# Seven-product column pairs in a SwiGLU layer: pinned weight sums on GpSimd, sums of h as side work, Silu on ScalarE

## The chip, the cores and the metric

The kernel runs on one core of a Trainium2 chip. The metric is device time in microseconds (us) of one execution, the median of several runs. A profile is taken of one execution; in it PE is the matrix engine, PEld its weight load, DVE the vector engine, ACT ScalarE, POOL GpSimd, SP the engine that issues the DMAs. Each engine takes its instructions in the order in which the program's scheduler has put them.

## The reference

Two layers of a hybrid trunk run over 576 tokens (512 of a prompt, 64 of a sample). Each layer has a token mixer (a state-space scan beside sliding-window attention), then a gated feed-forward part. Only the feed-forward part of the second layer (layer 1) matters here:

```
h2 = rmsnorm(x, norm_ffn_g) * (1 + sc_f) + sh_f          # 1024 x 576
gate, up = split(h2 @ w_gate_up, 2)                       # 2 x 2816 columns: 22 blocks of 128 each
x = x + gt_f * ((silu(gate) * up) @ w_down)
```

Everything is float32. A weight or an activation is split into a high part (the value rounded to the PE's faster float32 form) and a low part (what is left), and a product is three matmuls: high by high, low by high, high by low.

## The kernel before

**Tokens and weights.** The tokens are cut into two halves of 288 columns (`H0`, `H1`). A weight block (`Gran`, lines 172 to 200) is 1024 rows by 128 columns, 512 KB: SP loads it into one of four `raw` buffers, ACT casts the high part `whi` (line 168), DVE or POOL subtracts for the low part `wlo` (line 169, two instructions for a whole block; `eng` says on which engine). `whi` and `wlo` have four buffers each, and a `raw` buffer is free for the next load when both parts of the block stand.

**Classic blocks.** One column block f of gate and up takes 2 weight blocks x 2 halves x 8 k x 3 = 96 matmuls of 288 columns. `by_halves` runs the first half of several blocks ahead of their second half, with the weights loaded and split twice; the first three blocks of the feed-forward part (the lead: six jobs on H0, six on H1, 24 matmuls each) run so, since the second half of h2 is made while they run. That work is the side generator `nf1`: `Norm.apply` in four parts, each a scale on DVE, the shift on DVE and ACT, a cast on ACT (`hh`), a subtraction on DVE (`hl`).

**Pairs.** In layer 1 (`WIDE`) the other blocks are `PairJob`s (lines 350 to 393): gate and up columns of one f against the two halves are a 2 x 2 block product that is done with seven products in place of eight, 7 x 4 x 3 = 84 matmuls. It needs four sums of weight blocks per pair (`ws`, lines 227 to 232: s1, s2, s3, s4, all on POOL) and sums of the halves of h2 (T1 to T4, `Norm.combine`, lines 772 to 813), high and low part each. The products go in the order of step s = 0 to 6, and `step(s)` makes high and low part of the weights: s = 0, 4, 5 straight from `raw`, s = 1, 2, 3, 6 from s2, s3, s1, s4. The low part is made on POOL for s = 4 and 5 (`POOL_LO`), on DVE else. A pair's two `raw` buffers are given back after step 6.

**Sections.** The 22 blocks run in sections (`secs`), each followed by its share of w_down (8 output blocks, `dn`).

**Gates.** SiLU is built as (tanh(x/2) + 1) x on ACT and DVE, and the missing factor 1/2 stands in the adaLN gate (line 437).

**Order.** The code emits work job by job: weights of the next job are split after a job's first part, and side generators are advanced by `pump` at their rate at each step of a job. After that a scheduler orders the instructions of each engine by its own estimate, within the data's dependencies. So where an instruction stands in its engine's queue need not be where the code says it.

Of the kernel before, what the change touches and what calls it, by code (L numbers as in the profile page):

```python
# [12 lines left out]
ALU = mybir.AluOpType  # L13
# [38 lines left out]
def hybrid_trunk(ctx: ExitStack, tc: tile.TileContext, I, O):  # L52
# [109 lines left out]

    def f32(ap):
        return ap.bitcast(F32)
# [38 lines left out]
    class PairGran(Gran):  # L203
# [13 lines left out]
        def step(self, s):  # L217

            p = self.pair
            g, u = p["gate"], p["up"]  # L220
            if s == 0:
                p["s12"], p["s34"] = (w4("ws", [128, 2, 4, 128]) for _ in range(2))
                p["hi"], p["lo"] = [], []
            s1, s2 = p["s12"][:, 0], p["s12"][:, 1]
            s3, s4 = p["s34"][:, 0], p["s34"][:, 1]
            if s == 1:
                G.tensor_tensor(out=s1, in0=u.block(1, 0), in1=u.block(1, 1), op=ALU.add)  # L227
                G.tensor_tensor(out=s2, in0=s1, in1=g.block(0, 0), op=ALU.subtract)  # L228
            if s == 2:
                G.tensor_tensor(out=s3, in0=g.block(0, 0), in1=u.block(1, 0), op=ALU.subtract)  # L230
            if s == 6:
                G.tensor_tensor(out=s4, in0=g.block(0, 1), in1=s2, op=ALU.subtract)
# [187 lines left out]
    def ada_finish(l, b, ps):  # L420
# [15 lines left out]
        if b in (2, 5):  # L436
            V.tensor_scalar(out=md[:, b], in0=md[:, b], scalar1=0.5, scalar2=None, op0=ALU.mult)
# [261 lines left out]
    class Norm:  # L699
# [47 lines left out]
        def part(self, half, k2, src, fast):  # L747
# [21 lines left out]
            if self.wide and half:  # L769
                self.combine(k2, t)  # L770

        def combine(self, k2, t):

            js = slice(2 * (k2 % 2), 2 * (k2 % 2) + 2)
            if self.wino is None:
                self.wino = {}
                for n in range(4):
                    if n == 0:
                        v = [bcs("T", [128, 4, HALF], F32R) for _ in range(2)]
                    else:  # L780
                        v = blk("T", [128, 2, 4, HALF], F32R)
                        v = [v[:, 0], v[:, 1]]
                    self.wino[f"T{n + 1}"] = v
                for i in range(2):
                    for j in range(2):
                        self.wino[f"{i + 1}{j + 1}"] = [self.hh[i][:, :, HS[j]], self.hl[i][:, :, HS[j]]]

            def parts(nm):
                return [f32(a[:, js]) for a in self.wino[nm]]

            def less(x, nm, eng, sign=1):

                o = w4("tw", [128, 2, HALF])
                h, lo = parts(nm)
                if sign == 1:
                    eng.tensor_tensor(out=o, in0=x, in1=h, op=ALU.subtract)
                    eng.tensor_tensor(out=o, in0=o, in1=lo, op=ALU.subtract)
                else:
                    eng.tensor_tensor(out=o, in0=h, in1=x, op=ALU.subtract)
                    eng.tensor_tensor(out=o, in0=o, in1=lo, op=ALU.add)  # L800
                return o

            def put(nm, x, eng):
                h, lo = self.wino[nm]
                split(h[:, js], lo[:, js], x, eng)

            if k2 < 2:
                put("T1", less(t, "11", G), V)
                return
            t2 = less(t, "T1", V)  # L810
            put("T2", t2, V)
            put("T3", less(t, "12", G), G)
            put("T4", less(t2, "21", V, -1), V)
# [23 lines left out]
    def layer(l, nrm, jobs):  # L837
# [757 lines left out]
        secs = ((0, 4), (4, 6), (10, 6), (16, 6)) if wide else ((0, 8), (8, 8), (16, 6))  # L1595
# [8 lines left out]
        def a_alloc(f, f0, nf):  # L1604
# [11 lines left out]
        def pair_evac(f, f0, nf):  # L1616
            def evac(a, b, cc, d):
# [12 lines left out]
                act(g0, a, ACTF.Tanh, scale=0.5)  # L1630
                stt(g0, g0, 1.0, a, ALU.add, ALU.mult)
# [8 lines left out]
                act(g1, u2, ACTF.Tanh, scale=0.5)  # L1640
                stt(g1, g1, 1.0, u2, ALU.add, ALU.mult)
# [5 lines left out]
        def gu_evac(f, f0, nf):  # L1647
            def evac(m, half, ps):
                h = HS[half]
                if m == 0:  # L1650
                    t = st["gate", f, half] = w2("gate", [128, HALF])
                    act(t, ps[:, 0:HALF], ACTF.Tanh, scale=0.5)
                    stt(t, t, 1.0, ps[:, 0:HALF], ALU.add, ALU.mult)
                    return
# [43 lines left out]
        for sec, (f0, nf) in enumerate(secs):  # L1698
# [8 lines left out]
            if wide:  # L1707
                jobs += [PairJob(I["w_gate_up"][l], f, lambda: st["n2"], pair_evac(f, f0, nf), f)
                         for f in range(f0 + lead, f0 + nf)]
                if lead:  # L1710
                    jobs[-1].pre = lambda: drain("nf1")
# [163 lines left out]
```

## Time and profile before

| what | value |
|---|---|
| time of the runs | 2598.99 us, median of 3 (2594.55 to 2605.43) |
| the profiled execution | 2604.75 us, of which the span from first to last instruction is 2603.0 us |
| PE / DVE / POOL / ACT busy | 96% / 67% / 48% / 43% of the span |
| mean granted PE clock | 0.985 |

The feed-forward part of layer 1 runs from about 2141 us to the end. How to read it: matmuls of one product run into one another, so that a busy PE does not say at what rate they go; what counts is how many start in a stretch, how long PE waits and for whom, and the clock it was granted in that stretch (1.00 is 2.4 GHz, and 0.5 the other level, 1.2 GHz).

### The profile page before, as it was taken

The numbers are of one execution on the slowest core, as the hardware profiler recorded it, in microseconds if no ns is written. First come the engines' busy times: TensorE is split into PE (matmuls) and PEld (weight loads), VectorE is DVE, ScalarE is ACT, GpSimd is POOL, SyncE is SP. The second block draws the span as 40 slices with busy tenths as digits, with TensorE's granted clock in tenths as the row PEclk, the third lists the DMA queues.
The fourth block names the chain that finished last, engine by engine and source line by source line (L and its number), as shares of the span: only waits on it lengthen the run. The fifth ranks groups of instructions, "written<-read, shape, count | busy, mean of one in ns | idle before, by whom it ended". The sixth has DMA issues, their size and how long they took to land.

```text
span 2603.0 us, 49408 instructions
## 1 busy us (share of the span) xinstructions
PE 2508.9 (96%) x19381; PEld 2378.2 (91%) x19381; DVE 1737.2 (67%) x3159; ACT 1107.6 (43%) x2483; POOL 1244.4 (48%) x1092
## 2 busy tenths in 40 slices
PE   7999999999999999999999999999999997999989
PEld 6888899999889999999989899999988997998989
DVE  4598676745765765655768995956376567767684
ACT  3444454443453532322355455443354454333343
POOL 3445455343225754544675555544422378436260
PEclk8999999999999999999999999999999998999999
DMA  7555523242224555445573333323312253332323
GB/s 219 156 164 149 156 86 97 83 103 71 58 61 120 158 168 166 143 154 162 155 183 103 106 91 98 107 79 87 100 50 58 85 164 89 87 92 75 89 65 86
DMA packets 464236, 294.34 MB, mean 113 GB/s; under 512 B 69220, under 2 KB 446532, under 8 KB 464004
## 3 DMA queue, kind: packets, MB, share of 16 engines
q1 hardware_dynamic: 464004, 291.18, 38.9%
q8 instruction: 153, 2.51, 0.4%
q14 instruction: 79, 0.65, 0.1%
HBM read 276.98 MB, written 13.16 MB: 111 GB/s over the span
## 4 chain that ended last, share of the span: by engine, by line
PE 70%; DVE 15%; POOL 5%; DMA 5%; issue 3%; ACT 2%; SPq 0%; ACTq 0%; POOLq 0%; DVEq 0%
PE dps L326 19%; PE dps L328 19%; PE dps L327 19%; DVE cv L155 3%; POOL wlo L169 3%; DMA raw<-in_w_gate_up_dram 2%; DVE xT L155 2%; DVE seg L158 1%; PE sc L1353 1%; PE wps L371 1%; PE pv L1416 1%; PE wps L372 1%; PE wps L369 1%; POOL ws L228 1%; PE pT L1400 1%
## 5 line engine op out<-in xcount | busy, mean ns | idle before, releaser
L169 POOL TENSOR_TENSOR wlo<-raw,whi 128x512 fp32r<-128x512 f32 (+1 forms) x670 | 957.2, 1437 | 877.9 <-ACT whi L168 746.3
L326 PE MATMUL dps<-hh,whi 128*128 128x288 f32 x2928 | 878.6, 301 | 15.5 <-ACT whi L168 14.0
L327 PE MATMUL dps<-hh,wlo 128*128 128x288 f32 x2928 | 872.1, 298 | 2.8 <-POOL wlo L169 2.8
L328 PE MATMUL dps<-hl,whi 128*128 128x288 f32 x2928 | 871.4, 298 | 1.1 <-DVE hl L158 1.1
L168 ACT CAST whi<-raw 128x512 fp32r<-128x512 f32 (+2 forms) x759 | 453.7, 601 | 510.3 <-PE dps L328 366.7
L326 PEld LDWEIGHTS dps<-hh,whi 128*128 128x128 f32 x2928 | 552.3, 189 | 38.6 <-issue 16.8
L327 PEld LDWEIGHTS dps<-hh,wlo 128*128 128x128 f32 x2928 | 553.0, 189 | 12.0 <-POOL wlo L169 5.5
L328 PEld LDWEIGHTS dps<-hl,whi 128*128 128x128 f32 x2928 | 552.8, 189 | 7.7 <-issue 5.3
L155 DVE SCALAR_TENSOR_TENSOR ada_acc<-araw,csl,ada_acc 128x1024 f32<-128x1024 f32 x98 | 152.4, 1593 | 72.1 <-DMA araw<-in_ada_w_dram 72.1
L155 DVE SCALAR_TENSOR_TENSOR cv<-u,colB,cv 128x579 f32<-128x579 f32 x144 | 146.5, 1017 | 30.0 <-ACT cv L161 22.6
L326 PE MATMUL dps<-yh,whi 128*128 128x288 f32 x512 | 153.2, 299 | 1.1 <-ACT u L948 1.1
L328 PE MATMUL dps<-yl,whi 128*128 128x288 f32 x512 | 153.9, 301 | 0.0
L327 PE MATMUL dps<-yh,wlo 128*128 128x288 f32 x512 | 152.1, 297 | 0.0
L327 PE MATMUL dps<-ah,wlo 128*128 128x288 f32 x352 | 105.6, 300 | 4.1 <-POOL wlo L169 4.1
L326 PE MATMUL dps<-ah,whi 128*128 128x288 f32 x352 | 104.2, 297 | 3.2 <-ACT ah L168 2.6
L328 PE MATMUL dps<-al,whi 128*128 128x288 f32 x352 | 104.6, 297 | 0.0
L327 PE MATMUL dps<-a,wlo 128*128 128x288 f32 x352 | 104.4, 298 | 0.0
L326 PE MATMUL dps<-a,whi 128*128 128x288 f32 x352 | 103.1, 295 | 0.0
L328 PE MATMUL dps<-a,whi 128*128 128x288 f32 x352 | 102.8, 295 | 0.0
L227 POOL TENSOR_TENSOR ws<-raw 128x512 f32<-128x512 f32 x19 | 28.0, 1475 | 155.8 <-DMA raw<-in_w_gate_up_dram 145.2
L326 PEld LDWEIGHTS dps<-yh,whi 128*128 128x128 f32 x512 | 97.4, 190 | 4.1 <-issue 1.9
L155 DVE SCALAR_TENSOR_TENSOR x<-dps,mod,x 128x288 f32<-128x288 f32 (+2 forms) x168 | 63.6, 411 | 54.1 <-PE dps L328 52.6
(372 smaller groups left out, 5484.4 us busy)
## 6 DMA issues: line engine op xcount, KB each, us to landing
raw<-in_w_in_dram SPq DMA_DIRECT2D x119, 512.0 KB
raw<-in_w_gate_up_dram SPq DMA_DIRECT2D x100, 512.0 KB
araw<-in_ada_w_dram SPq DMA_DIRECT2D x56, 512.0 KB
bc<-ac_dr SPq DMA_DIRECT2D x32, 512.0 KB
raw<-in_w_br_ssm_dram SPq DMA_DIRECT2D x32, 512.0 KB
raw<-in_w_out_dram SPq DMA_DIRECT2D x32, 512.0 KB
raw<-in_w_down_dram SPq DMA_DIRECT2D x40, 384.0 KB
raw<-in_ada_w_dram SPq DMA_DIRECT2D x24, 512.0 KB
```

Of the source, the lines that this page charges most:

```text
L155: V.scalar_tensor_tensor(out=out, in0=in0, scalar=scalar, in1=in1, op0=op0, op1=op1)
L158: V.tensor_tensor(out=out, in0=in0, in1=in1, op=op)
L168: S.copy(out=hi, in_=src)
L169: (eng or V).tensor_tensor(out=lo, in0=src, in1=f32(hi), op=ALU.subtract)
L227: G.tensor_tensor(out=s1, in0=u.block(1, 0), in1=u.block(1, 1), op=ALU.add)
L228: G.tensor_tensor(out=s2, in0=s1, in1=g.block(0, 0), op=ALU.subtract)
L326: T.matmul(ps, lhsT=wh, rhs=rh, start=a == 0, stop=False)
L327: T.matmul(ps, lhsT=wl, rhs=rh, start=False, stop=False)
L328: T.matmul(ps, lhsT=wh, rhs=rl, start=False, stop=a == nk - 1)
L369: T.matmul(ps, lhsT=wh[:, k], rhs=rh[:, k], start=first and k == 0, stop=False, skip_group_check=True)
L371: T.matmul(ps, lhsT=wl[:, k], rhs=rh[:, k], start=False, stop=False, skip_group_check=True)
L372: T.matmul(ps, lhsT=wh[:, k], rhs=rl[:, k], start=False, stop=k == 3, skip_group_check=True)
```

## The change

Four edits, all in layer 1's feed-forward part.

1. The four weight sums are put through `tc.keep_in_program_order`, so that the scheduler leaves them where the code emits them on POOL.
2. The sums of h are no longer made inside `Norm.part`. `combine` is a generator of its own, made from `hh` and `hl` (three GpSimd instructions for T3 and for T1, two on DVE for T2 and for T4, and the splits), added as side work `comb` (rate 0.75) when the H1 jobs of the lead begin and drained before the first pair.
3. Two more blocks (f = 3 and 4) are classic, and the sections are cut 6, 6, 6, 4 in place of 4, 6, 6, 6. The weights of the six H1 jobs of the lead are split on DVE in place of POOL.
4. In layer 1 the gate is one Silu on ACT, without the DVE instruction behind Tanh and without the factor 1/2.

```diff
+    pin = tc.keep_in_program_order
...
             if s == 1:
-                G.tensor_tensor(out=s1, in0=u.block(1, 0), in1=u.block(1, 1), op=ALU.add)
-                G.tensor_tensor(out=s2, in0=s1, in1=g.block(0, 0), op=ALU.subtract)
+                pin(G.tensor_tensor(out=s1, in0=u.block(1, 0), in1=u.block(1, 1), op=ALU.add))
+                pin(G.tensor_tensor(out=s2, in0=s1, in1=g.block(0, 0), op=ALU.subtract))
...
-            if self.wide and half:
-                self.combine(k2, t)
...
+        def combine(self):
...
+            for js in (slice(0, 2), slice(2, 4)):
+                part = lambda nm: [f32(a[:, js]) for a in self.wino[nm]]
...
+                def less(p, q, eng):
+                    (ph, pl), (qh, ql) = part(p), part(q)
+                    o, r = (w4("tw", [128, 2, HALF]) for _ in range(2))
+                    eng.tensor_tensor(out=o, in0=ph, in1=qh, op=ALU.subtract)
+                    eng.tensor_tensor(out=r, in0=pl, in1=ql, op=ALU.subtract)
+                    eng.tensor_tensor(out=o, in0=o, in1=r, op=ALU.add)
+                    return o
+
+                t3 = less("22", "12", G)
+                put("T3", t3, V)
+                yield
+                (h, lo), t2 = part("11"), w4("tw", [128, 2, HALF])
+                tt(t2, t3, h, ALU.add)
+                tt(t2, t2, lo, ALU.add)
+                put("T2", t2, G)
+                yield
+                (h, lo), t4 = part("21"), w4("tw", [128, 2, HALF])
+                tt(t4, h, t2, ALU.subtract)
+                tt(t4, t4, lo, ALU.add)
+                put("T4", t4, G)
+                yield
+                put("T1", less("12", "11", G), V)
+                yield
...
-        secs = ((0, 4), (4, 6), (10, 6), (16, 6)) if wide else ((0, 8), (8, 8), (16, 6))
+        secs = ((0, 6), (6, 6), (12, 6), (18, 4)) if wide else ((0, 8), (8, 8), (16, 6))
...
+        def gate(out, x):
+
+            if wide:
+                act(out, x, ACTF.Silu)
+                return
+            act(out, x, ACTF.Tanh, scale=0.5)
+            stt(out, out, 1.0, x, ALU.add, ALU.mult)
...
+                if lead:
+                    f1 += 2
+                    for j in gj[2 * lead:]:
+                        for gr in j.gr:
+                            gr.eng = V
+                    gj[2 * lead].pre = lambda: (drain("nf1"), add_side("comb", st["n2"].combine(), 0.75))
+                    jobs += gu_jobs(range(f0 + lead, f1))
+                pj = [PairJob(I["w_gate_up"][l], f, lambda: st["n2"], pair_evac(f, f0, nf), f)
+                      for f in range(f1, f0 + nf)]
+                if lead:
+                    pj[0].pre = lambda: drain("comb")
```

What the scheduler makes of it, first on POOL, among the pairs of one section. In the program before, rows of two pairs in a row (`ws` are the sums s1, s3, s2, s4, `wlo` the low parts of steps 4 and 5; the numbers tell buffers apart, so that raw_26504 and raw_26506 are gate and up of one pair, raw_26340 and raw_26379 of the pair before it):

```order
L227 TENSOR_TENSOR ws_26539<-raw_26379 128x512
L230 TENSOR_TENSOR ws_26540<-raw_26340,raw_26379 128x512
L228 TENSOR_TENSOR ws_26539<-ws_26539,raw_26340 128x512
L232 TENSOR_TENSOR ws_26540<-raw_26340,ws_26539 128x512
L169 TENSOR_TENSOR wlo_26463<-raw_26262,whi_26462 128x512
L169 TENSOR_TENSOR wlo_26482<-raw_26301,whi_26481 128x512
L227 TENSOR_TENSOR ws_26686<-raw_26506 128x512
L230 TENSOR_TENSOR ws_26687<-raw_26504,raw_26506 128x512
L228 TENSOR_TENSOR ws_26686<-ws_26686,raw_26504 128x512
L232 TENSOR_TENSOR ws_26687<-raw_26504,ws_26686 128x512
L169 TENSOR_TENSOR wlo_26613<-raw_26340,whi_26612 128x512
L169 TENSOR_TENSOR wlo_26632<-raw_26379,whi_26631 128x512
```

The low parts of one pair stand behind all four sums of the next pair. In the changed program the same engine at the same place, two pairs in a row (raw_26666 and raw_26717, then raw_26860 and raw_26862):

```order
L229 TENSOR_TENSOR ws_26894<-raw_26717 128x512
L230 TENSOR_TENSOR ws_26894<-ws_26894,raw_26666 128x512
L232 TENSOR_TENSOR ws_26895<-raw_26666,raw_26717 128x512
L171 TENSOR_TENSOR wlo_26967<-raw_26666,whi_26966 128x512
L171 TENSOR_TENSOR wlo_26986<-raw_26717,whi_26985 128x512
L234 TENSOR_TENSOR ws_26895<-raw_26666,ws_26894 128x512
L229 TENSOR_TENSOR ws_27039<-raw_26862 128x512
L230 TENSOR_TENSOR ws_27039<-ws_27039,raw_26860 128x512
L232 TENSOR_TENSOR ws_27040<-raw_26860,raw_26862 128x512
L171 TENSOR_TENSOR wlo_27112<-raw_26860,whi_27111 128x512
L171 TENSOR_TENSOR wlo_27131<-raw_26862,whi_27130 128x512
L234 TENSOR_TENSOR ws_27040<-raw_26860,ws_27039 128x512
```

Each pair's six instructions now stand together: s1, s2, s3, the two low parts, s4, and then the next pair's.

Second on DVE, where the lead goes from its H0 to its H1 jobs. Before (`nt2` is h2 in the making, `hl` its low part, `tw` and `T` the sums of h, `gate` and `a` the activation of a lead block):

```order
L158 TENSOR_TENSOR nt2_25611<-x_24756,bc_25437 128x576
L158 TENSOR_TENSOR hl_25050<-nt2_25550,hh_25048 128x2x288
L765 TENSOR_SCALAR nt2_25611<-nt2_25611,mod1_2490 128x64
L760 TENSOR_SCALAR nt2_25611<-nt2_25611,mod1_2490 128x224
L765 TENSOR_SCALAR nt2_25611<-nt2_25611,mod1_2490 128x64
L155 SCALAR_TENSOR_TENSOR gate_25697<-gate_25697,dps_25672 128x288
L169 TENSOR_TENSOR T_25450<-tw_25454,T_25449 128x576
L796 TENSOR_TENSOR tw_25558<-nt2_25550,T_25449 128x576
L158 TENSOR_TENSOR hl_25050<-nt2_25611,hh_25048 128x2x288
L797 TENSOR_TENSOR tw_25558<-tw_25558,T_25450 128x576
```

After, the same place (`wlo` here are low parts of the first H1 jobs' weights):

```order
L158 TENSOR_TENSOR nt2_25579<-x_24755,bc_25436 128x576
L171 TENSOR_TENSOR wlo_25691<-raw_25532,whi_25690 128x512
L158 TENSOR_TENSOR hl_25049<-nt2_25534,hh_25047 128x2x288
L767 TENSOR_SCALAR nt2_25579<-nt2_25579,mod1_2490 128x64
L762 TENSOR_SCALAR nt2_25579<-nt2_25579,mod1_2490 128x224
L767 TENSOR_SCALAR nt2_25579<-nt2_25579,mod1_2490 128x64
L171 TENSOR_TENSOR wlo_25695<-raw_25532,whi_25694 128x512
L171 TENSOR_TENSOR wlo_25728<-raw_25577,whi_25727 128x512
L158 TENSOR_TENSOR gate_25650<-gate_25650,dps_25662 128x288
L158 TENSOR_TENSOR hl_25049<-nt2_25579,hh_25047 128x2x288
```

The last `hl` of h2 now has three weight splits ahead of it in place of a gate instruction, a T and a tw; all sums of h stand behind it. On POOL, where four subtractions of 576 columns stood among the weight splits at this place, the first sum of h now stands behind the last low part of the H0 jobs. Ahead of 2141 us all five queues are ordered as before, save one small DVE instruction (the factor 1/2) that is gone.

## Rows read from the trace of the kernel before

**Rows 1.** The page's first line
```profile
span 2603.0 us, 49408 instructions
```

**Rows 2.** Stretches of layer 1's feed-forward: length, busy us (count) by engine, clock, DMA
```profile
2141.00:2204.00 63.00, 47.65 (x311) 45.06 (x309) 47.72 (x59) 28.22 (x56) 56.68 (x39) 0.89 0.33 95
...
2237.00:2309.00 72.00, 64.15 (x451) 62.89 (x450) 58.24 (x84) 30.80 (x61) 45.69 (x31) 0.95 0.27 76
2309.00:2369.00 60.00, 60.00 (x455) 60.00 (x454) 35.62 (x73) 20.32 (x41) 17.35 (x13) 1.00 0.32 93
2369.00:2422.00 53.00, 43.76 (x317) 42.74 (x316) 41.32 (x60) 22.72 (x46) 35.30 (x24) 0.98 0.24 68
2422.00:2486.00 64.00, 64.00 (x479) 64.00 (x478) 38.94 (x77) 21.67 (x43) 17.39 (x13) 0.99 0.32 93
2486.00:2541.00 55.00, 46.78 (x317) 45.34 (x316) 45.19 (x61) 22.46 (x46) 35.41 (x24) 0.92 0.24 69
```

**Rows 3.** PE's pair matmuls from 2141 us, one of each three like groups
```profile
L371 PE MATMUL wps<-T,wlo 128*128 128x288 f32 x304 | 92.8, 305 | 0.9 <-POOL wlo L169 0.6 <-DVE wlo L169 0.3
...
L371 PE MATMUL wps<-hh,wlo 128*128 128x288 f32 x228 | 69.9, 307 | 24.7 <-POOL wlo L169 24.7
```

**Rows 4.** PE's waits from 2141 to 2204.5 us: total, times, longest
```profile
PE dps L326 <- ACT whi L168: 13.4, 6, 5.7
PE dps L327 <- POOL wlo L169: 1.1, 2, 0.7
```

**Rows 5.** PE's waits from 2204.5 us to the end
```profile
PE wps L371 <- POOL wlo L169: 25.3, 14, 3.1
```

**Rows 6.** PE at one wait, then at the lower clock: start, duration
```profile
2258.18 0.29 PE L369 MATMUL wps<-hh,whi 128*128 128x288 f32 x1
2261.57 0.40 PE L371 MATMUL wps<-hh,wlo 128*128 128x288 f32 x1 [3.09 <-POOL wlo L169]
...
2264.10 0.44 PE L371 MATMUL wps<-T,wlo 128*128 128x288 f32 x1
2264.34 0.44 PE L372 MATMUL wps<-T,whi 128*128 128x288 f32 x1
```

**Rows 7.** POOL over the same pair: start, duration, [idle before]
```profile
2253.83 1.61 POOL L227 TENSOR_TENSOR ws<-raw 128x512 f32<-128x512 f32 x1 [5.26 <-DVE gate L155]
...
2259.81 2.95 POOL L169 TENSOR_TENSOR wlo<-raw,whi 128x512 fp32r<-128x512 f32 x2
2267.53 1.44 POOL L227 TENSOR_TENSOR ws<-raw 128x512 f32<-128x512 f32 x1 [4.77 <-DMA raw<-in_w_gate_up_dram]
```

**Rows 8.** POOL's sums and low parts from 2237 to 2309 us: busy, mean ns
```profile
L169 POOL TENSOR_TENSOR wlo<-raw,whi 128x512 fp32r<-128x512 f32 x10 | 14.8, 1504 | 0.0
...
L228 POOL TENSOR_TENSOR ws<-ws,raw 128x512 f32<-128x512 f32 x5 | 8.2, 1650 | 0.0
```

**Rows 9.** DVE's low parts of weights, 2237 to 2309 us: min/median/max ns
```profile
L169 DVE TENSOR_TENSOR wlo<-ws,whi x22: 677/692/1787, 2239.0 to 2308.1; 128x512 fp32r<-128x512 f32 x22
...
L169 DVE TENSOR_TENSOR wlo<-raw,whi x6: 677/1342/1541, 2237.0 to 2305.7; 128x512 fp32r<-128x512 f32 x6
```

**Rows 10.** DVE by form, 2141 to 2204 us, the slowest sum of h
```profile
L800 DVE TENSOR_TENSOR tw<-tw,hl 128x576 f32<-128x576 f32 x2 | 3.7, 1854 | 0.0
```

**Rows 11.** ACT: the one table load (1.3 us busy), and the first lead gate
```profile
L161 ACT ACT_TABLE_LOAD x1 | 1.3, 1283 | 0.8 <-PEq L1860 0.8
...
2145.41 0.41 ACT L161 ACTIVATE gate<-dps 128x288 f32<-128x288 f32 x1 [0.91 <-PE dps L328]
...
2147.71 0.62 ACT L168 CAST whi<-raw 128x512 fp32r<-128x512 f32 x1 [1.37 <-POOL wlo L169]
```

**Rows 12.** DVE at the end of h2's second half: start, duration
```profile
2162.21 1.41 DVE L760 TENSOR_SCALAR nt<-nt,mod 128x224 f32<-128x224 f32 x1
...
2169.60 0.30 DVE L765 TENSOR_SCALAR nt<-nt,mod 128x64 f32<-128x64 f32 x1
...
2171.53 1.83 DVE L158 TENSOR_TENSOR hl<-nt,hh 128x576 fp32r<-128x576 f32 x1
```

More of the change, by code (lines that the diff above doesn't have):

```diff
@@ L435, in ada_finish @@
                 ALU.add, ALU.mult)
-        if b in (2, 5):
+        if b == 2 or b == 5 and l not in WIDE:
             V.tensor_scalar(out=md[:, b], in0=md[:, b], scalar1=0.5, scalar2=None, op0=ALU.mult)
@@ L768, in part @@
             tt(self.hl[q][:, ks, h], t, f32(hi), ALU.subtract)
-            if self.wide and half:
-                self.combine(k2, t)
[L772 to L797, printed above, removed]
-                else:
[L799 to L813, printed above, removed]
@@ new lines, in combine, with put @@
+        def combine(self):
+            self.wino = {}
+            for n in range(4):
+                if n == 0:
+                    v = [bcs("T", [128, 4, HALF], F32R) for _ in range(2)]
+                else:
+                    v = blk("T", [128, 2, 4, HALF], F32R)
+                    v = [v[:, 0], v[:, 1]]
+                self.wino[f"T{n + 1}"] = v
+            for i in range(2):
+                for j in range(2):
+                    self.wino[f"{i + 1}{j + 1}"] = [self.hh[i][:, :, HS[j]], self.hl[i][:, :, HS[j]]]
+            for js in (slice(0, 2), slice(2, 4)):
+                part = lambda nm: [f32(a[:, js]) for a in self.wino[nm]]
+                def put(nm, x, eng):
+                    h, lo = self.wino[nm]
+                    split(h[:, js], lo[:, js], x, eng)
+                def less(p, q, eng):
[20 more added lines that the diff above has]
+                yield
@@ L1629, in evac @@
                 g0 = w2("gate", [128, HALF])
-                act(g0, a, ACTF.Tanh, scale=0.5)
-                stt(g0, g0, 1.0, a, ALU.add, ALU.mult)
+                gate(g0, a)
                 yield
@@ L1639, in evac @@
                 g1 = w2("gate", [128, HALF])
-                act(g1, u2, ACTF.Tanh, scale=0.5)
-                stt(g1, g1, 1.0, u2, ALU.add, ALU.mult)
+                gate(g1, u2)
                 tt(g1, g1, u3, ALU.mult)
@@ L1651, in evac @@
                     t = st["gate", f, half] = w2("gate", [128, HALF])
-                    act(t, ps[:, 0:HALF], ACTF.Tanh, scale=0.5)
-                    stt(t, t, 1.0, ps[:, 0:HALF], ALU.add, ALU.mult)
+                    gate(t, ps[:, 0:HALF])
                     return
@@ L1707, in layer @@
             if wide:
-                jobs += [PairJob(I["w_gate_up"][l], f, lambda: st["n2"], pair_evac(f, f0, nf), f)
-                         for f in range(f0 + lead, f0 + nf)]
+                f1 = f0 + lead
                 if lead:
-                    jobs[-1].pre = lambda: drain("nf1")
+                    f1 += 2
[8 more added lines that the diff above has]
+                    pj[0].pre = lambda: drain("comb")
+                jobs += pj
             else:
```

4 lines of the change are left out of this document (2 added, 2 removed).

## The prediction

> **What bounds the kernel now.** I read the stretches of the feed-forward part first, then PE's instructions in it, PE's waits, and last what the engines that PE waits for were doing. The part begins at 2141 us and ends with the span at 2603.0 [rows 1], so it takes 462.0. Two stretches show PE undisturbed: 455 matmuls in 60 us at a clock of 1.00 and 479 in 64 us at 0.99 [rows 2], together 124 / 934 = 0.1328 us per matmul. The pairs hold 304 x 3 + 228 x 3 = 1596 = 19 x 84 matmuls [rows 3]; by the code the lead adds 3 x 96 = 288 and w_down 22 x 8 x 2 x 3 = 1056. That is 2940, or 390.4 us. The other 71.6 us are the room. The waits of PE account for 13.4 + 1.1 in the lead [rows 4] and 25.3 in the pairs [rows 5], 39.8 in all. The clock accounts for more: at 0.89 over 63 us, the lower level held 2 x 0.11 x 63 = 13.9 us, and 7.2, 2.1, 1.3 and 8.8 in the other stretches, 33.3 together [rows 2]. At that level matmuls start 0.24 apart in place of 0.133 [rows 6], so that each such microsecond loses 0.45: 14.9. It fell after PE had waited (as after the 3.09 us ahead of these rows), and stood at 1.00 and 0.99 in the two stretches without a wait. Each wait also costs more than its length: from 2258.18 to 2261.57 are 3.39, less 0.13 for the matmul, 3.26 for a wait of 3.09 [rows 6]; 0.17 x 22 waits = 3.7. What remains, 71.6 - 39.8 - 14.9 - 3.7 = 13.2, is the end of the kernel, the transposes of the output and smaller things, and I leave it as it is.
>
> **The pairs' waits: a loop.** All 14 are for a low part made on POOL. POOL takes 13.70 us from one pair's first sum to the next one's (2253.83 to 2267.53): four sums, 5.98; two low parts, 2.95; then 4.77 idle until the weights land [rows 7]. These weights could not be loaded earlier, since their `raw` buffers are free only after the low parts, and the low parts stand behind the next pair's sums, which wait for weights. PE needs 84 x 0.1328 = 11.16 per pair, so the loop sets the pace.
>
> **The pins.** With the new order the low parts wait for nothing but their own high parts. I walk one pair, from the start of its first product, a product being 12 x 0.1328 = 1.59; a cast takes 0.62 [rows 11], POOL's low part 1.50 and its slowest kind of sum 1.65 [rows 8]. The buffer of step 4 is free at 1.59, cast at 2.2, low part at 3.7. Step 5: free at 3.19, cast at 3.8, low part at 5.3, needed only at 8.0. Then s4 at 6.95, its cast at 7.6, its low part on DVE (0.69 to 1.34, [rows 9]) by 8.3 to 8.9. Product 6 wants it at 6 x 1.59 + 0.13 = 9.7. Four hand-overs between engines may take 0.5 of the slack (my estimate), which leaves none or 0.9. The `raw` buffers come free at about 7, and 4.77 later the weights of the pair after next are there, 6 us before they are asked for. s4 is thus what is late next, and it just fits. I take 2 us of waits for all 17 pairs; the bounds are 0, and 10 if the walk is 0.6 late each time. From 25.3 to 2: **-23.3**.
>
> **The lead.** The 1.1 at its start comes before anything that moves and stays. PE then waits for casts that stand behind h2's second half in ACT's queue, and that half is held up on DVE: its shifts take 1.41 while POOL works beside them and 0.30 when it does not, and its last low part ends at 2171.53 + 1.83 = 2173.4 [rows 12]. PE without further waits would be through with the first H1 job at 2141 + 7 x 24 x 0.1328 + 2 (the 1.1, and small matmuls of the norm) = 2165. In the new order three instructions ahead of that low part are gone (0.45 to 0.75 each, about 1.9) and POOL's four subtractions beside it too, which lets some five shifts fall by 1 us each; three weight splits come in, 0.69 to 1.34 each, say 3. So 2173.4 - 1.9 - 5 + 3 = 2169.5, and with the six matmuls that need this part (0.8) the job ends at 2170.3: 5 us of waits. For the five jobs that follow, DVE has 9 splits, 2 parts of T, 4 sums of h and 4 gate instructions. At 0.69 for all but the gates (0.45) this is 12 us; at 1.34 per split and 1.85 per sum or T [rows 9, 10] and 0.8 per gate instruction, 26. PE's own time is 5 x 24 x 0.1328 = 15.9. I take the middle, 19; the first splits are done while PE waits for that last low part, so 2 us of waits. Sum 1.1 + 5 + 2 = 8, with bounds 2 and 20: **-6.5**. The rest of comb lies beside f = 3 and 4, where a weight block serves 6.4 us of PE in place of 3.2; POOL's 16 instructions (24 us at 1.50) end before the first pair wants them.
>
> The Trainium skill has a rule that speaks against this part: in "SBUF — State Buffer", section "SBUF: two separate sides", a DVE instruction with two inputs in SBUF and a GpSimd one exclude each other for the whole instruction. The trace agrees in kind, but the median split on DVE from `ws` shows no delay [rows 9]. By the rule's full price the lead is rival A.
>
> **Two more classic blocks.** 2 x (96 - 84) = 24 matmuls more, **+3.2**. The order of the sections changes no count. In the last one an output block has 24 matmuls in place of 36; its loads shrink with it (nk = 4 of 128 rows in place of 6), so nothing.
>
> **Silu.** Its activation is put at Tanh's 0.41 [rows 11]; as the upper bound the 0.62 of a cast of 512 columns, as the lower one no gain. Even 0.62 adds 0.4 us per pair to an engine that is 45% busy at most [rows 2], so nothing. DVE loses two small instructions per pair. The table is loaded once more, ahead of the first lead gate at 2145.41: 1.28 us, with 1.37 idle soon behind it [rows 11]. Hence 0, and 1.3 if that idle time is not to be had.
>
> By the Trainium skill, "ScalarE: Activation LUTs", section "What ACT_TABLE_LOAD costs", a switch is 2.66 us, the same load with a drain behind it; the sum would be up to 1.3 us higher. The row shows the load alone.
>
> **Clock and restarts.** They go with the waits: 10 of 39.8 are left, so the clock keeps 14.9 x 0.25 = 3.7 (**-11.2**; bounds 1 and 13), the restarts 1 (**-2.7**).
>
> **Sum.** 3.2 - 23.3 - 6.5 - 11.2 - 2.7 = -40.5. The profiled execution took 2604.75, 5.8 above the median of 2598.99 that the result will be held against; I take the difference from the median: 2558.5, rounded to 2558. All the low bounds together give 3.2 - 25.3 - 12.5 - 13.9 - 3.5 = -52, 2547; all the high ones give 3.2 - 15.3 + 5.5 - 1.9 - 0.5 + 1.3 = -8, 2591.
>
> **Rivals.**
> A, DVE becomes the bound of the lead. For it: 9 splits and 6 sums of h land on DVE while POOL works without a break; against it, the median of 0.69. If each of the 15 waits for a whole POOL instruction of 1.50, the five jobs take 15 x 2.19 + 4 x 0.45 = 34.7, 18.8 of waits, 24 for the lead. Then 26 us of waits remain, the clock keeps 9.7 and the restarts 2: 3.2 - 23.3 + 9.5 - 5.2 - 1.7 = -17.5, 2581.
> B, s4 is late. If POOL's instructions take 1.9, s4's low part comes about 0.5 late in each of 17 pairs: 8.5 of waits there, clock 6, restarts 3: 3.2 - 16.8 - 6.5 - 9 - 0.7 = -30, 2569.
> C, the weights are the bound and the pins only move the wait from the low parts to the sums. For it: POOL does wait 4.77 for a landing. Against it: a pair's 1 MB in 11.16 us is 94 GB/s, and 95 GB/s were moved in the lead with a DMA share of 0.33 [rows 2]. If the pair stays at 13.7, 22.6 of the 25.3 remain: 3.2 - 2.7 - 6.5 - 3.4 - 1 = -10, 2589.
> D, slower: six POOL instructions per pair are a chain by themselves now that s4 may not run ahead. It decides from about 2.3 us each, where six take 13.8, the loop's length now. At 2.6 a pair takes 15.6, PE waits 17 x 4.4 = 75 where it waited 25.3, and with the clock's part the end is some 60 later, 2660. Against it: means of 1.50 and 1.65 [rows 8].
>
> **How the numbers follow.** Forecast 0.66, A 0.15, B 0.09, C 0.06, D 0.04. What a measurement of this kernel can tell from no change is about 0.5%, 13 us, 2586 to 2612. Faster: forecast, A and B, 0.90; same: C, 0.06; slower: D, 0.04. The forecast's own range is 2545 to 2571; to hold A's place too the range is 2543 to 2583.
>
> **What would show it.** Right: no wait of PE on POOL's low parts over 1 us in the pairs, POOL no longer idle for a DMA ahead of a pair's first sum, pairs 11.2 to 11.5 apart, a clock of 0.98 or more from the first pair on, and PE at the first pair's product at about 2141 + 63.7 + 9 = 2214. Wrong: waits of PE on a DVE low part once per pair (B), long DVE splits in the lead with PE waiting for DVE (A), or pairs 13 us apart (C, D).

## The result, and the profile after

The changed kernel takes 2560.9 us (median of four runs, 2556.5 to 2563.4) where the kernel before, on the same chip, took 2600.7: a ratio of 0.985, with a 95% interval of 0.982 to 0.987. The forecast was 2558. The profiled execution took 2562.08, its span 2560.3, against 2604.75 and 2603.0.

In that execution the part before the change ran 2.8 us shorter, in the same order: PE's last matmul ahead of the lead's first wait starts at 2138.28, where it was 2141.06. I count from there: 461.9 before, 422.0 after, 39.9 less. By the prediction's terms:

| term | predicted | measured |
|---|---|---|
| waits in the pairs | -23.3 | -23.8 (25.3 to 1.5) |
| waits in the lead | -6.5 | -5.9 (14.5 to 8.6) |
| two more classic blocks | +3.2 | +3.2 (by count: 24 matmuls more) |
| clock | -11.2 | -13.3 (33.3 us at the lower level to 3.8, at 0.45 each) |
| end, behind PE's last matmul | 0 | +1.9 (4.36 to 6.26) |
| restarts, and all that is left | -2.7 | -2.0 (the remainder) |
| sum | -40.5 | -39.9 |

The waits of PE in the changed kernel from 2141 us on (line and tile, what it waited for, total, times, longest; one more of 0.7 for POOL lies at 2139):

```profile
PE dps L329 <- DVE wlo L171: 7.9, 6, 2.3
PE wps L373 <- DVE wlo L171: 1.5, 7, 0.2
```

The line of 25.3 us for POOL's low parts [rows 5] is gone, with nothing of its size in its place. Seven small waits of the pairs are now for DVE. The stretches (columns as in [rows 2]):

```profile
span 2560.3 us, 49363 instructions
...
2141.00:2188.00 47.00, 39.16 (x275) 37.57 (x273) 41.83 (x50) 24.15 (x46) 36.02 (x23) 0.96 0.43 124
...
2225.00:2290.00 65.00, 65.00 (x491) 64.90 (x490) 39.96 (x74) 22.31 (x45) 21.40 (x15) 1.00 0.32 91
2290.00:2325.00 35.00, 34.35 (x252) 33.38 (x251) 27.48 (x43) 16.71 (x37) 26.74 (x18) 1.00 0.30 84
2325.00:2397.00 72.00, 72.00 (x544) 71.90 (x543) 44.88 (x83) 25.93 (x53) 25.76 (x18) 1.00 0.32 92
...
2504.00:2560.00 56.00, 49.77 (x378) 48.95 (x376) 30.43 (x67) 21.07 (x53) 13.27 (x9) 0.97 0.28 81
```

The clock stood at 1.00 from 2188 to 2504; only the lead has time at the lower level, 2 x 0.04 x 47 = 3.8 us (the 0.97 of the last stretch comes from 2554 us on, where PE has all but ended). The DMAs moved 124 GB/s in the lead, where pairs need 84 to 92.

POOL over one pair (start, duration, idle before and its releaser), the place of [rows 7]:

```profile
2290.26 3.09 POOL L171 TENSOR_TENSOR wlo<-raw,whi 128x512 fp32r<-128x512 f32 x2 [2.76 <-ACT whi L170]
2293.31 1.29 POOL L234 TENSOR_TENSOR ws<-raw,ws 128x512 f32<-128x512 f32 x1
2294.56 1.28 POOL L229 TENSOR_TENSOR ws<-raw 128x512 f32<-128x512 f32 x1
...
2302.01 3.08 POOL L171 TENSOR_TENSOR wlo<-raw,whi 128x512 fp32r<-128x512 f32 x2 [2.76 <-ACT whi L170]
```

The two low parts come first, then s4 and the next pair's sums. Between the pairs of a section the wait for a landing is gone: POOL waits for ACT's cast. It waits for a landing only ahead of a section's first pair, while PE works on w_down: three times from 2225 us on, and PE waits for none of them. The low parts start 11.75 us apart, where the pair of [rows 7] took 13.70.

### The profile page after: what moved, and what is told of

The parts are those of the page before. It is cut to its first block, busy times and chain, and to the rows that moved or that the text cites. A ratio compares the mean times of both kernels' runs of the same rounds, so it can differ in the third digit from the quotient of the medians.

```text
span 2560.3 us, 49363 instructions
## 1 busy us (share of the span) xinstructions
PE 2496.8 (98%) x19405; PEld 2368.0 (92%) x19405; DVE 1701.0 (66%) x3112; ACT 1098.6 (43%) x2476; POOL 1217.6 (48%) x1074
## 4 chain that ended last, share of the span: by engine, by line
PE 70%; DVE 16%; POOL 5%; issue 5%; DMA 2%; ACT 2%; SPq 0%; ACTq 0%; POOLq 0%; DVEq 0%
PE dps L328 19%; PE dps L330 19%; PE dps L329 19%; DVE cv L155 3%; POOL wlo L171 3%; DVE xT L155 2%; PE sc L1354 1%; DVE seg L158 1%; PE pv L1417 1%; DVE wlo L171 1%; PE pT L1401 1%; PE sp L1067 1%; DVE ada_acc L155 1%; DVE hl L158 1%; DVE nt L158 1%
## 5 line engine op out<-in xcount | busy, mean ns | idle before, releaser
L171 POOL TENSOR_TENSOR wlo<-raw,whi 128x512 fp32r<-128x512 f32 (+1 forms) x654 | 932.0, 1434 | 932.4 <-ACT whi L170 827.6
L329 PE MATMUL dps<-hh,wlo 128*128 128x288 f32 x2992 | 889.8, 298 | 10.4 <-DVE wlo L171 7.9
L328 PE MATMUL dps<-hh,whi 128*128 128x288 f32 x2992 | 895.0, 300 | 2.0 <-ACT hh L769 1.4
L330 PE MATMUL dps<-hl,whi 128*128 128x288 f32 x2992 | 888.8, 297 | 1.4 <-DVE hl L158 1.4
L328 PEld LDWEIGHTS dps<-hh,whi 128*128 128x128 f32 x2992 | 562.7, 188 | 23.7 <-issue 16.0
L329 PEld LDWEIGHTS dps<-hh,wlo 128*128 128x128 f32 x2992 | 563.5, 188 | 20.6 <-DVE wlo L171 9.5
L330 PEld LDWEIGHTS dps<-hl,whi 128*128 128x128 f32 x2992 | 563.6, 188 | 7.9 <-issue 5.3
L171 DVE TENSOR_TENSOR wlo<-raw,whi 128x384 fp32r<-128x384 f32 (+2 forms) x101 | 86.2, 859 | 30.7 <-ACT whi L170 30.5
L330 PEld LDWEIGHTS dps<-yl,whi 128*128 128x128 f32 x512 | 96.6, 189 | 2.0 <-issue 1.8
```

The lines of the kernel that those rows point to most:

```text
L171: (eng or V).tensor_tensor(out=lo, in0=src, in1=f32(hi), op=ALU.subtract)
L328: T.matmul(ps, lhsT=wh, rhs=rh, start=a == 0, stop=False)
L329: T.matmul(ps, lhsT=wl, rhs=rh, start=False, stop=False)
L330: T.matmul(ps, lhsT=wh, rhs=rl, start=False, stop=a == nk - 1)
```

## The experiments

Five columns to compare them. The runs come from several chips, each beside runs of the kernel before on the same chip, so that medians of different kernels compare less well than ratios. "From 16,300" is the time from one matmul ahead of the lead, number 16,300 of the program, to the end of the span, in each profiled execution: it leaves out what happens ahead of the change (474.2 for the kernel before). "To the end" is the time from PE's first product of a pair to the end of the span, in each profiled execution; it is free of what happens ahead of the pairs, and kernels that are alike there agree in it within 0.4 us (345.2, 345.0, 345.3 and 344.9 for the changed kernel and three that differ in the lead alone). Pairs are from POOL's rows where they are evenly spaced, the pace of the loop. PE's own pairs reach that pace late: in the changed kernel a section's six pairs start 11.15, 11.14, 11.27, 11.75 and 11.75 apart.

| kernel | median us | ratio (interval) | from 16,300 | to the end | pairs |
|---|---|---|---|---|---|
| changed kernel | 2560.9 | 0.9846 (0.9820 to 0.9872) | 434.3 | 345.2 | 11.75 |
| pins alone | 2576.5 | 0.9902 (0.9883 to 0.9920) | 450.3 |  | 11.96 |
| no pins | 2585.2 | 0.9938 (0.9923 to 0.9953) | 458.8 | 369.7 |  |
| Tanh | 2565.1 | 0.9863 (0.9848 to 0.9877) | 436.7 | 347.3 | 11.97 |
| three classic blocks | 2571.2 | 0.9888 (0.9873 to 0.9903) | 444.3 |  |  |
| first splits on POOL | 2563.9 | 0.9857 (0.9836 to 0.9877) | 436.7 | 345.0 |  |
| all splits on POOL | 2563.8 | 0.9859 (0.9838 to 0.9879) | 437.9 | 344.9 |  |
| comb later | 2558.8 | 0.9840 (0.9819 to 0.9862) | 433.5 | 345.3 |  |
| step 6 on POOL | 2577.1 | 0.9907 (0.9887 to 0.9928) | 450.5 | 359.9 | 12.64 |
| cast later | 2559.5 | 0.9838 (0.9822 to 0.9854) | 434.2 | 343.6 | 11.62 |
| gate later | 2558.1 | 0.9839 (0.9815 to 0.9863) | 434.0 | 343.5 | 11.44 |
| four yo buffers | 2559.5 | 0.9847 (0.9833 to 0.9860) | 432.7 | 343.6 |  |
| gate later, four yo | 2557.7 | 0.9835 (0.9821 to 0.9850) | 430.1 | 341.1 | 11.44 |

**Pins alone.** The kernel before with the pins:
```
-  G.tensor_tensor(out=s1, in0=u.block(1, 0), ...)
+  pin(G.tensor_tensor(out=s1, in0=u.block(1, 0), ...))     # and s2, s3, s4
```


> The kernel before with the four pins alone. Theory (the loop of low parts, loads and sums is what the pins break): the pairs' waits on POOL fall from 25.3 to about 2, the lead keeps its 14.5, the clock gives back 8.7 of 14.9 and the restarts 2.4; 2603.0 - 34.7 is 2568 of span, ratio 0.987. Rival (the pins help only where the lead's edits have unloaded DVE and POOL): the pairs keep most of their waits, ratio above 0.995.

It came to 0.9902; from matmul 16,300 on the trace is 23.9 us shorter, where 34.7 was expected. PE's waits in that kernel (1.1 for POOL in the lead is not shown), and the stretches at its lead and behind it:
```profile
PE dps L328 <- ACT whi L170: 12.4, 5, 4.5
PE wps L373 <- DVE wlo L171: 2.2, 10, 0.3
PE wps L371 <- ACT whi L170: 2.0, 2, 1.5
```
```profile
2140.00:2208.00 68.00, 52.42 (x310) 50.23 (x309) 50.51 (x59) 28.88 (x56) 56.34 (x38) 0.82 0.30 88
2208.00:2260.00 52.00, 51.67 (x378) 51.54 (x378) 33.67 (x74) 19.74 (x43) 17.54 (x13) 0.97 0.32 92
```
The pairs' waits fell as foreseen, and the lower level went with them there: the stretch behind the lead holds 3.1 us of it and what follows none, where the pairs of the kernel before held 33.3 - 13.9 = 19.4 [rows 2]. But the lead now holds 2 x 0.18 x 68 = 24.5 us in place of 13.9, so that 27.6 of 33.3 remain in all. Of the 10.8 us that are missing, the clock makes 6: it gives back 2.6 in place of 8.7.

**No pins.** The changed kernel with
```
-    pin = tc.keep_in_program_order
+    pin = lambda i: i
```


> The changed kernel without the pins. Theory: the sums stand ahead of the low parts again, a pair takes 13.7, PE waits about 22 in 17 pairs for POOL's low parts, and with clock and restarts the time is some 31 over the changed kernel: 2592, ratio 0.997. Rival (the lead's edits and Silu brought the gain): within 5 of the changed kernel, ratio below 0.987.

0.9938, between theory and rival: the pins are worth 458.8 - 434.3 = 24.5 us here, nearly what they are worth alone, and 0.9902 x 0.9938 = 0.984 is the whole change. So the two parts simply add. PE's waits, and the stretches of the lead and of those pairs that ran in part at the lower level:
```profile
PE wps L373 <- POOL wlo L171: 19.1, 10, 3.0
PE dps L329 <- DVE wlo L171: 7.9, 6, 2.3
```
```profile
2137.00:2188.00 51.00, 42.39 (x296) 40.69 (x296) 44.76 (x55) 27.55 (x52) 38.52 (x25) 0.97 0.41 118
...
2290.00:2340.00 50.00, 43.48 (x293) 42.69 (x292) 29.98 (x48) 20.10 (x41) 27.05 (x19) 0.90 0.26 74
...
2436.00:2500.00 64.00, 61.38 (x452) 61.14 (x451) 35.36 (x69) 19.84 (x39) 21.02 (x16) 0.97 0.28 83
...
2526.00:2540.00 14.00, 11.22 (x73) 10.99 (x72) 7.18 (x13) 5.43 (x11) 6.03 (x5) 0.88 0.14 39
```
The loop is back with its waits, 19.1 us in 17 pairs, and so is the lower level in the pairs: 10.0 + 3.8 + 3.4 = 17.2 us in these three stretches, none in the others; the lead holds 3.1. So the lower level lies in the stretch in which PE waits: the pins take it out of the pairs (19.4 to 3.1 in the kernel before, 17.2 to none here), the other edits out of the lead (13.9 to 3.1 without pins, 24.5 to 3.8 with them). How much of it goes with a microsecond of wait is not fixed: 0.9 in these pairs, 0.4 in the changed kernel's lead (3.8 for 8.6), 1.6 in the lead and first pair of pins alone (24.5 for 12.4 + 1.1 + 2.0). Each is from one profile.

**Tanh.** The changed kernel with the gate as before (the factor 1/2 in the adaLN gate is back too, and not shown here):
```
-            if wide:
-                act(out, x, ACTF.Silu)
-                return
             act(out, x, ACTF.Tanh, scale=0.5)
```


> The changed kernel with the gate as before (Tanh on ACT, one more DVE instruction, the factor 1/2). Theory: nothing on the path hangs on it, 2559 to 2563, ratio 0.984 to 0.986. Rival (two DVE instructions per pair and four per lead block are on the path): 17 pairs x 2 x 0.4 = 14 us slower, ratio 0.990.

The interval of its ratio overlaps that of the changed kernel; the trace tells more. Pairs are 11.97 apart in place of 11.75, and the stretch to the end is 2.1 longer. Silu is worth some 2 us in these traces; the likely cause, not tested by itself, is that it takes two instructions off DVE, which is in the pairs' loop. The table's load was paid by nobody: PE has no wait for ACT in the changed kernel's lead (ACT there, start and duration):
```profile
2141.72 1.28 ACT L161 ACT_TABLE_LOAD   x1
2143.02 0.41 ACT L161 ACTIVATE gate<-dps 128x288 f32<-128x288 f32 x1
```
The gate takes 0.41 with Silu as it did with Tanh, and starts 0.02 behind the load.

**Three classic blocks.** f = 3 and 4 as pairs again, comb as side work beside whatever there is:
```
                 if lead:
-                    f1 += 2
```


> The changed kernel with f = 3 and 4 as pairs. Theory: 24 matmuls less (-3.2), but PE is at the first pair at about 2188 in place of 2214, while POOL has the sums of h behind it only at 2200 and the first pair's sums of weights at 2205; PE waits 12 to 17 there, the clock and restarts take 3 more: about 2573 to 2577, ratio 0.990. Rival (the sums of h hide beside any work): 2558, ratio 0.984.

0.9888, as its theory had it: 10.3 us behind the changed kernel by the medians and 10.0 in the trace, though it has 24 matmuls (3.2 us) fewer. The two largest waits of PE up to 2214 us, and the stretch in which they lie:
```profile
PE wps L371 <- ACT whi L170: 7.8, 2, 6.2
PE wps L371 <- ACT T L170: 4.4, 1, 4.4
```
```profile
2180.00:2214.00 34.00, 18.87 (x105) 16.90 (x104) 20.76 (x24) 10.96 (x20) 26.32 (x18) 0.70 0.14 39
```
PE reaches the first pair at 2180.6, stands before sums and T that POOL and ACT have not made yet, and 2 x 0.30 x 34 = 20.4 us then run at the lower level. In the changed kernel comb ends at 2200.5 and the first product starts at 2215.1. The two blocks are the cover for comb.

**Who makes the splits of the second half.** Two kernels: the splits of its first two jobs, and of all its jobs, on POOL in place of DVE (the first kernel's edit, then the second's):
```
-                    for j in gj[2 * lead:]:
+                    for j in gj[2 * lead + 2:]:
```
```
-                            gr.eng = V
+                            gr.eng = G
```


> The changed kernel with the low parts of the first two H1 jobs' weights on POOL, the other four jobs' on DVE. Theory (PE's first waits in the lead, 1.4 + 2.3 + 0.7 between 2159 and 2167, are for splits that queue in DVE among h2's own instructions, while POOL is idle half of that time): they shrink to 1 to 2, 3 us are won, comb ends 4 to 6 us later and still ahead of the first pair: 2556 to 2559, ratio 0.983 to 0.984. Rival (POOL beside DVE slows the shifts of h2 again, to 1.4 from 0.3, as before): the wait only changes its name, 2561 or more.

> The changed kernel with all six H1 jobs' splits on POOL, as before the change. Theory: POOL has 12 splits (17 us) more in the lead, comb's three-instruction sums are pushed back as far, and the sums of the first pair come at about 2222 where PE wants them at 2214: 5 to 8 us of waits at the first pair beside 5 to 10 in the lead, 2566 to 2572, ratio 0.987 to 0.989. Rival (who splits does not matter, comb alone brought the lead's gain): 2561, ratio 0.9845.

Both are 3 us behind the changed kernel by the medians, and their intervals overlap with its own. The waits change their names and hardly their length. With all splits on POOL:
```profile
PE dps L328 <- ACT whi L170: 4.1, 2, 3.5
PE dps L328 <- ACT hh L769: 2.4, 1, 2.4
PE dps L329 <- POOL wlo L171: 1.8, 2, 1.0
PE dps L329 <- DVE wlo L171: 1.6, 1, 1.6
```
9.9 us, where DVE's splits left 8.6. I had expected comb to end too late; it ended at 2206.9 (at 2200.5 in the changed kernel, whose trace runs 1.8 us behind), and the first pair at 2217.2 still found its sums. The traces say a little more than the medians: from matmul 16,300 to the first pair's product these two kernels take 91.7 and 93.0 us, where the seven with the changed kernel's lead take 89.1 or 90.6. So by these two profiles the splits on DVE are worth 1 to 4 us.

**Comb later.**
```
-  gj[2 * lead].pre = lambda: (drain("nf1"), add_side("comb", ...))
+  gj[2 * lead + 3].pre = lambda: add_side("comb", ...)    # nf1 is not drained here any more
```


> The changed kernel with comb added three H1 jobs later. Theory (DVE's splits of 1.5 to 1.9 between 2175 and 2186, and PE's 3.4 of waits there, come from POOL working beside them): these waits go, the splits there take 0.7; but comb ends some 8 later and the first pair waits 2 to 5 for it: 2559 to 2563. Rival (DVE simply has too many instructions there): the waits in the lead stay at 8 and the first pair's come on top, 2564 or more.

This tells nothing: the scheduler put the first sum of h at the same place in POOL's queue (2156.4 in a trace that runs 2.5 us ahead, 2158.9 in the changed kernel), so DVE was not relieved of POOL. How much of the lead's 8.6 us is DVE held up by POOL stays open.

**Step 6 on POOL.** The wait that is left in the pairs is for DVE's low part. Give POOL the one of s4 as well:
```
-    POOL_LO = (4, 5)
+    POOL_LO = (4, 5, 6)
```


> The changed kernel with the low part of step 6 on POOL as well. In the changed kernel a pair takes 11.74, not 11.16, by a loop: step 6's and step 0's low parts on DVE, the gate product, ACT's cast behind it in the queue of casts, steps 4 and 5 and s4 on POOL, step 6's cast. Theory (that loop, bound by DVE's 1.1 for step 6): a low part less on DVE but 1.5 more on POOL ahead of the next pair's sums, so the loop is no shorter and s2 is late: pairs 12 to 12.5, 2566 to 2574, ratio 0.987 to 0.990. Rival (DVE's load alone sets the 0.58): pairs 11.2 to 11.4, 2555 to 2558.

Pairs 12.64 apart, PE waits 12.1 us, 16 us slower: the theory's direction, a little beyond its range. POOL in this kernel:
```profile
2300.43 1.29 POOL L171 TENSOR_TENSOR wlo<-ws,whi 128x512 fp32r<-128x512 f32 x1 [0.73 <-ACT whi L170]
2301.68 1.75 POOL L229 TENSOR_TENSOR ws<-raw 128x512 f32<-128x512 f32 x1
```
The next pair's sums now stand behind the low part's 1.3 us and its 0.73 of idling. So these sums are in the loop, and POOL has no room for this low part.

**Cast later.** What else is in it? In the changed kernel ACT idles once per pair on a cast of the gated product, with two casts behind it, one of which has had its input since 2307.6 and the other since 2311.0 (start, duration, idle before):
```profile
2309.33 0.62 ACT L170 CAST whi<-ws 128x512 fp32r<-128x512 f32 x1 [1.51 <-POOL ws L230]
2311.34 0.44 ACT L170 CAST a<-nt 128x288 fp32r<-128x288 f32 x1 [1.39 <-DVE nt L158]
2311.68 1.14 ACT L170 CAST whi<-ws 128x512 fp32r<-128x512 f32 x2
```
The experiment puts that cast one step later:
```
                 tt(t, t, g0, ALU.mult)
-                split(hi[:, H0], lo[:, H0], t)
                 yield
                 ...
                 gate(g1, u2)
+                pin(S.copy(out=hi[:, H0], in_=t))      # and its low part on DVE
```


> The kernel after, with one move: in each pair the cast of the first half of the gated product (a, from nt) and its low part stand one step later in ACT's and DVE's queue, behind the casts of s2's and s3's blocks and the second gate, where they stood ahead of them. In the kernel after ACT waits 1.39 us for nt at this place while two casts that have their input stand behind it, and pairs are 11.74 us apart. Theory (that cast is a link of the loop that keeps pairs at 11.74): pairs 11.2 to 11.5 apart, no gap of 0.37 to 0.39 us at the ninth pair's place of each section, PE waits of 17 pairs some 4 to 7 us less, 2554 to 2557 us, ratio 0.982 to 0.983. Rival 1 (the loop runs over POOL and DVE alone, the cast is only a bystander): pairs stay at 11.7, same time as the kernel after, ratio 0.9845. Rival 2 (the later a comes too late for w_down): a new wait of PE on a at the start of each w_down stage, 2562 or more.

11.62: the cast is a link, but only 0.13 us of it counts; 11.2 to 11.5 was too much. ACT in this kernel, ahead of the low parts that POOL starts at 2300.60:
```profile
2299.23 0.45 ACT L161 ACTIVATE gate<-u 128x288 f32<-128x288 f32 x1
2299.58 0.42 ACT L1648 CAST a<-nt 128x288 fp32r<-128x288 f32 x1
2299.90 0.62 ACT L170 CAST whi<-raw 128x512 fp32r<-128x512 f32 x1
```
The cast for POOL still stands behind a gate and another cast.

**Gate later.** So these go behind it too:
```
             u.step(4)
+            late and next(late.pop())     # second gate, a-casts of the pair before
             product(1, b, True)
...                                               # `late` takes each pair's last piece of work
```


> The cast-later kernel with one more link taken out of ACT's queue: the second gate of a pair, its product, the cast of the second half of a (and the late cast of the first half) stand behind the cast of the next pair's step 4, where that cast stood behind them. In the cast-later kernel the cast of step 4 starts at 2299.90, 1.0 us after PE began the product that shows its buffer free (2298.89), because ACT runs the gate and the a-cast first, and POOL's low part starts behind it. Theory (the loop is PE, then ACT's cast of step 4, POOL's two low parts and s4, ACT's cast of step 6, DVE's low part of step 6 and what DVE does behind it up to the next low part): POOL starts 0.6 to 1.0 us earlier within a pair, pairs fall from 11.61 to 11.16 to 11.3, the seven waits of PE on DVE's low part are gone or under 0.1, PE waits 1 us less, 2555 to 2558 us, ratio 0.982 to 0.983. Rival (DVE's own work per pair beside POOL is the bound, whatever ACT's order): POOL starts earlier and idles longer, pairs stay at 11.6, 2559 to 2561, ratio 0.984.

11.44, and the seven waits are gone. One of 1.06 us, for DVE's u, has come in their place (PE's waits):
```profile
PE dps L329 <- DVE wlo L171: 9.4, 6, 2.3
PE wps L372 <- DVE u L158: 1.1, 1, 1.1
```
The whole does not show it (0.9839): only some ten pairs are evenly spaced at the loop's pace, the new wait takes back what they give (343.5 to the end, as in the kernel before this one), and this execution's lead was 1.5 us longer, with a stretch at the lower level from 2188 on.

**Four yo buffers.** The end behind PE's last matmul had grown by 1.9 us, which no term of mine foresaw. ACT's last copies of the output in the changed kernel:
```profile
2552.91 0.59 ACT L1695 COPY yo<-xo 128x512 f32<-128x512 f32 x1 [2.99 <-PE xo L1693]
...
2555.99 0.59 ACT L1695 COPY yo<-xo 128x512 f32<-128x512 f32 x1 [2.33 <-DMA out_dram<-yo]
```
The last copy waits for an earlier output to land, for its buffer; five copies of the last section do, 7.0 us in all. Before, all eight waited for PE: an output block took 36 matmuls, 4.8 us, and now 24, 3.2 us.
```
-                yo = wt("yo", [128, 512])      # two buffers
+                yo = w4("yo", [128, 512])      # four
```


> The kernel after, with four buffers for the output copies (yo) in place of two. In the kernel after the last section has 24 matmuls per output block in place of 36, its blocks end every 3.2 us, and ACT's copy of an output block waits for the landing of an earlier one five times (7.0 us, the last one 2.33); from PE's last matmul to the end of the span are 6.26 us, where the kernel before took 4.36. Theory (the buffer's wait is what makes the end 1.9 longer): no copy of ACT waits for a landing, PE's end to span's end 4.3 to 4.6, the part 1.7 to 1.9 us shorter, about 2559 us, ratio 0.983 to 0.984, which the trace's end and not the ratio has to show. Rival (the output's transfers themselves are the bound at this pace): the wait moves to the transfers, the end stays at 6.0 to 6.3.

The landing is gone from ACT's waits (`issue`: the profile shows nothing that ACT waited for):
```profile
2547.63 0.59 ACT L1695 COPY yo<-xo 128x512 f32<-128x512 f32 x1 [2.99 <-issue]
...
2548.99 0.59 ACT L1695 COPY yo<-xo 128x512 f32<-128x512 f32 x1 [0.62 <-ACT yo L1699]
```
From PE's last matmul to the end are 4.55 us in place of 6.26. That is too little for the ratio, and enough for the trace.

**Both.** The gate-later kernel with the four buffers:

> The gate-later kernel (pairs at 11.45 us) and the four yo buffers together. If both savings hold and add (1.3 to 2.5 us in the pairs, 1.8 at the end): 2556 to 2558 us, ratio 0.982 to 0.983, with the lead's waits of 8 to 9 us as they were. Rival (the end or the pairs give it back): 2560 or more, ratio 0.9845.

PE's waits from 2135 us on, all but one of 0.3 at the output, and the stretch of the pairs:
```profile
PE dps L329 <- DVE wlo L171: 7.9, 6, 2.3
PE dps L329 <- POOL wlo L171: 0.7, 1, 0.7
```
```profile
2188.00:2504.00 316.00, 316.00 (x2368) 314.23 (x2368) 229.78 (x357) 125.25 (x254) 152.69 (x102) 1.00 0.30 88
```
PE has no wait left in the pairs, and the stretch to the end is 341.1, 4.1 less than in the changed kernel. Its median of 2557.7 is the lowest of all; its interval overlaps that of the changed kernel, so that it is the faster of the two is shown by the stretch and not by the ratio.

## Why the prediction was right, and where only its sum was

**The pairs' loop: right.** The low parts stood behind sums that waited for weights, and turning them round took the landing out of the loop. The marks came as named: no wait of PE for POOL in the pairs, POOL waiting for ACT's cast where it waited for a DMA (save ahead of a section's first pair), and 1.00 from the first pair on. The no-pins kernel shows the cause: without the pins the loop and its 19.1 us of waits come back. One mark came by luck: the first pair's product stood at 2215.1 where 2214 was foretold, but this execution ran 2.8 us ahead. Counted from the same matmul it came 76.8 us on and not 72.9. The mark had left out the lower clock and the restarts; the rest of the way to the end then took 345.2, where the sum had left 348.5.

**The walk of a pair: a little too kind.** It gave 11.2 to 11.5 and had s4's low part late by nothing. The loop's pace is 11.75, which PE's pairs reach from the fourth of a section on, and PE waits 0.2 seven times, for DVE. That is the sign that was named for rival B, but not its cause: the low part that is late is that of s2, for step 1 of the next pair, and not s4's. It costs 1.5 us in all where B had 8.5. The walk followed one chain and left out what stands ahead of its links in the same queues. DVE in the changed kernel:
```profile
2307.03 1.12 DVE L171 TENSOR_TENSOR wlo<-ws,whi 128x512 fp32r<-128x512 f32 x1 [1.40 <-ACT whi L170]
2308.07 1.77 DVE L171 TENSOR_TENSOR wlo<-raw,whi 128x512 fp32r<-128x512 f32 x1
2309.77 0.44 DVE L158 TENSOR_TENSOR nt<-u,wps 128x288 f32<-128x288 f32 x1
2310.31 0.99 DVE L158 TENSOR_TENSOR nt<-nt,gate 128x288 f32<-128x288 f32 x1
2311.23 0.68 DVE L171 TENSOR_TENSOR wlo<-ws,whi 128x512 fp32r<-128x512 f32 x1
```
The low part of s4 takes 1.12 and the next pair's first one 1.77 beside POOL's sums, then come the gate's product and only then the low part of s2, which PE waits for from 2311.75 to 2311.96. Behind it ACT's gate and casts hold up POOL's low parts, and POOL's s4 holds up DVE again. The two kernels that shortened ACT's piece brought 11.62 and 11.44, and Tanh, which lengthens DVE's, 11.97. What keeps it at 11.44, 0.3 over PE's 11.16, was not tried.

**The lead: the size right, the place partly.** 8.6 us of waits against 8. h2's second half was through on DVE at 2168.0, against 2169.5 foretold; counted from the same matmul that is 1.3 later and not earlier. But the waits are for low parts of weights, 4.4 us in the first job and 3.5 in those that follow, where I had 5 and 2. These splits are slow where POOL works beside them (DVE, and POOL's sum of h beside the second split):
```profile
2167.29 0.75 DVE L158 TENSOR_TENSOR hl<-nt,hh 128x576 fp32r<-128x576 f32 x1
2167.96 0.68 DVE L171 TENSOR_TENSOR wlo<-raw,whi 128x512 fp32r<-128x512 f32 x1
...
2176.57 1.95 POOL L797 TENSOR_TENSOR tw<-tw 128x576 f32<-128x576 f32 x1
2177.15 1.92 DVE L171 TENSOR_TENSOR wlo<-raw,whi 128x512 fp32r<-128x512 f32 x1
...
2180.60 3.72 DVE L171 TENSOR_TENSOR wlo<-raw,whi 128x512 fp32r<-128x512 f32 x2
```
The split of 2177.15 began while POOL's sum was running and ended 0.55 behind it; POOL was idle beside the one of 2167.96. This is rival A's mechanism for some 15 us, not for all of the lead; no run takes it out by itself. The rule that the Trainium skill gives in "SBUF — State Buffer", section "SBUF: two separate sides", that a DVE instruction with two inputs in SBUF and a GpSimd one exclude each other, agrees with the 1.9 in place of 0.68 here.

**The clock: nearly the right size, by a rule that holds only roughly.** -13.3 against -11.2. I had shared it out in proportion to the waits, by which the pins would have been worth 23.3 + 8.8 + 2.1 = 34 and the rest of the change 6. The traces give 24 for the pins, alone or on top, and 15 to 16 for the rest. "They go with the waits" is right as to the place, for the lower level lies where PE waits, and too simple as to the amount, which went from 0.4 to 1.6 us of it per microsecond of wait. The other half of the error is that the parts overlap in the waits too: without the pins the other edits already bring the pairs' waits from 25.3 to 19.1, and take 10.8 us of the lower level out of the lead.

**Two more classic blocks: priced as cost alone.** Their 24 matmuls cost 3.2 us, and without them the kernel is 10.3 us slower. I had counted their cover within the lead's term and never asked what the lead would be without them.

**Silu: nothing foretold, about 2 us measured.** "An engine that is 45% busy" says nothing of an instruction that stands in a loop of queues.

**The last section: "nothing" was wrong by 1.9 us.** Its loads shrink with its blocks, but its outputs do not: each block still sends as much out, in two thirds of the time, through two buffers.

A, C and D did not come: the lead waited 8.6 and not 24, POOL waits for no landing between the pairs of a section, and its six instructions took 1.28 to 1.74 each.

## What to carry to other kernels

When one engine's queue holds work of two stages, look for an instruction that is ready behind one that waits for a transfer: turning them round took away nearly the whole wait here (25.3 us to 1.5), and the next limit is the same pattern one engine on (here ACT's casts, for 0.3 us per pair). Price a lower clock stretch by stretch, for it lay where PE waited, but not at one rate per microsecond of wait, and price cover by what stands bare without it. And when a stage is made shorter, follow its outputs too: buffers that were never waited for are sized for the old pace.

## What the runs showed that I had not expected

Ahead of the change, 2130 us of the same instructions in almost the same order differ from run to run by more than most edits here move: one matmul of the layer before the lead (number 16,300) starts anywhere from 2120.6 to 2128.8 in the fourteen traces, with no pattern by kernel, while the 345 us behind the first pair's product repeat within 0.4. Part of that may be the chip, but four traces from one chip still span 2123.6 to 2127.5. A stretch measured in the trace resolved 2 us where five rounds of whole runs resolve 4 to 6.

With the pins alone the lead held more of the lower level than before (24.5 us against 13.9 [rows 2]), though its waits were the same to 1 us. That is the larger part of what the pins alone fell short by, and one profile each does not tell whether it is chance.
